# State-space mixer of a two-layer decoder step: outputs by chunk with rows of 64, weights that run on, slots inside the scan

## The chip, the cores and the metric

The kernel runs on one core of one Trainium2 chip. The metric is the device time of one execution in microseconds (us), as the median of several runs.

## What is computed

One inference step of a two-layer decoder, all in fp32, over 288 tokens (a prompt of 256 and 8 sample sequences of 4) and 16 learned meta tokens. Layer 0 mixes tokens with a gated short convolution, layer 1 with a diagonal complex state-space mixer (S5) and a gated linear unit (GLU); each layer ends in an MLP with a squared ReLU. The part that matters here is the mixer of layer 1:

```python
bu_re = jnp.einsum('btgc,gpc->btgp', u32, bbar_re)
bu_im = jnp.einsum('btgc,gpc->btgp', u32, bbar_im)
cum_ar, cum_ai, cum_br, cum_bi = lax.associative_scan(
    _scan_combine, (a_re, a_im, bu_re, bu_im), axis=1)
...
y = (jnp.einsum('gcp,btgp->btgc', c_re, h_re)
     - jnp.einsum('gcp,btgp->btgc', c_im, h_im)
     + d_skip.reshape(SSM_GROUPS, SSM_GROUP_WIDTH) * u32)
g = jax.nn.gelu(y.reshape(bsz, L, D_MODEL))
out = (g @ w_a) * jax.nn.sigmoid(g @ w_b)
```

There are 128 groups of 16 channels, 64 complex states each; `w_a` and `w_b` are 2048 x 2048.

## The kernel before, in words

Activations lie transposed: 16 tiles of 128 channels, with the tokens along the free dimension (304 columns, 288 without the meta tokens). Tokens come in chunks of four, 76 chunks, and the state-space mixer works on chunks: a tile holds 8 groups, as 4 pairs `q` of two groups.

**Weights.** Every dense product takes its weights from one stream, `WeightStream` (lines 41 to 77). A slot is 2 k-tiles by 512 columns, 512 KB: a DMA on the SP queue into one of 4 `raw` buffers (L55), a rounded copy `whi` on ScalarE (L66), the remainder `wlo` on VectorE (L68), 3 buffers of each, then 24 matmuls on TensorE (L200 to L202). `take()` prepares 2 slots ahead and loads 4 more. `W.limit` is the last slot that may be loaded: before the mixer it is set to the end of layer 0's MLP (L1147), and lifted at L1213, once the mixer has begun.

**The mixer**, per tile `t` of 16. `st_m1` (L1036): 8 fp32 matmuls of 128x128 by 76 columns bring the inputs into state space. `st_samples` (L1051, L1052): two small copies on ScalarE. `st_scan` on VectorE: rotate (L1064, L1065, L1067), scan (L1069), rotate back (L1071, L1072, L1074, L1076); `between(k)` puts other work between these steps. `st_y`: 16 fp32 matmuls (L1101, with the tile's inputs) and 32 (L1106, with its states), each with 32 columns of weights that write one strip of 32 partitions of `ybank`, so that the outputs come out with channels on partitions. Then ScalarE takes the gelu (L1113) and its rounded part (L1116), VectorE the remainder (L1117).

**Early slots.** While the tiles run, GLU slots are taken as soon as their k-tiles exist: `run_slots(PERSTEP)` takes up to 2 per tile, after the whole scan and ahead of `st_y`. A slot is gated by `ready`, the number of tiles whose gelu is written. `EARLY` lists the groups and how many k-tiles each takes there: 27 of the 64 GLU slots; the other 37 (`LATE`) follow the mixer.

The order is written by hand: each engine, and each DMA queue, works through its instructions in the program's order.

```python
    for t in range(NT):
        st_samples(t)
        ...
        st_scan(t, between)
        run_slots(PERSTEP)
        lo_of_tile.append(st_y(t))
    lo_of_tile.pop()()
    ready[0] = NT
    run_slots(99)
    st_scan_samples()
```

Of the kernel before, what the change touches and what calls it, by code (L numbers as in the profile page):

```python
# [79 lines left out]
def build(ctx, tc, I, O, dbg=None):  # L80
    nc = tc.nc
    V, S, G, T = nc.vector, nc.scalar, nc.gpsimd, nc.tensor
# [866 lines left out]
    ssm = {}  # L949
    gh = [None, None]  # L950

    def ssm_alloc():
# [3 lines left out]
        blk = xr[:, 0:5120].rearrange("p (n m) -> p n m", m=P)
        ssm["m1"] = [blk[:, 8 * i:8 * i + 8, :] for i in range(2)]
        ssm["m2"] = [blk[:, 16 + 8 * i:24 + 8 * i, :] for i in range(2)]
        ssm["tt"] = [blk[:, 32 + 4 * i:36 + 4 * i, :] for i in range(2)]
        ssm["rot"] = [xr[:, 5120 + i * 816:5120 + (i + 1) * 816] for i in range(3)]  # L960
        ssm["tmp"] = [xr[:, 7568 + i * 544:7568 + (i + 1) * 544] for i in range(3)]
        sel = ssm["sel"] = xr[:, 9200:9712].rearrange("p (j m) -> p j m", j=4)
# [9 lines left out]
        G.memset(xr[:, 0:5120], 0.0)  # L972
# [110 lines left out]
    def st_scan_samples():  # L1083
# [10 lines left out]
    def st_y(t):  # L1094

        def cols_of(ap, i):
            return ap.rearrange("p (x i) -> p x i", i=4)[:, :, i]

        for i in range(4):
            for q in range(4):  # L1100
                T.matmul(out=ybank[32 * q:32 * q + 32, i * NK:(i + 1) * NK], lhsT=cols_of(ssm["tt"][t % 2][:, q, :], i),  # L1101
                         rhs=ssm["U"][:, t * 4 + q, :], start=i == 0, stop=False)
        for r in range(2):
            for i in range(4):
                for q in range(4):
                    T.matmul(out=ybank[32 * q:32 * q + 32, i * NK:(i + 1) * NK],  # L1106
                             lhsT=cols_of(ssm["m2"][t % 2][:, q * 2 + r, :], i), rhs=ssm["S"][t % 2][:, q, r, :],
                             start=False, stop=r == 1 and i == 3)
# [107 lines left out]

    for t in range(NT):
        st_samples(t)

        def between(k):  # L1220
            if k == 0:
                if t + 1 < NT:
                    st_m1(t + 1)
                if t == 0:
                    W.dma_to(W.idx + NRAW)
                while lo_of_tile:
                    lo_of_tile.pop()()
                    ready[0] = t
            elif k == 1 and t + 2 < NT:
                scale_u(t + 2)  # L1230
            elif k == 2 and t < 2:
                W.prep_to(W.idx + 1 + t)
# [121 lines left out]
```

## Time and profile before

| | |
|---|---|
| median of 3 runs | 2567.64 us (2564.65 to 2569.97) |
| the profiled execution's own time | 2565.84 us |
| its span in the trace | 2563.8 us |
| mean granted TensorE clock | 0.973 |
| busy: TensorE, VectorE, ScalarE, GpSimd | 95%, 60%, 37%, 5% |

Line numbers (L200) are those of the kernel before, unless the text says of the kernel after; PE is TensorE's matmuls, PEld its weight loads, DVE VectorE, ACT ScalarE, POOL GpSimd, SP the engine whose queue issues most DMAs. An idle time in brackets stands ahead of an instruction, with what ended it; "issue" means that the trace shows nothing that was waited for. A fp32 matmul shows as two records of PE, a transposition and a matmul on split weights (fp32r) as one.

### The profile page before, as it was taken

How to read it: one execution, taken by the hardware profiler on the slowest of the kernel's cores; microseconds unless marked ns; L12 is line 12 of the kernel's file. 1: busy time of each engine (PE TensorE's matmuls, PEld its weight loads, DVE VectorE, ACT ScalarE, POOL GpSimd, SP SyncE). 2: the span in 40 equal slices, each digit the busy share in tenths (PEclk: the TensorE clock that was granted, in tenths of full speed). 3: DMA queues.
4: the chain of work that ended last, by engine and by line, in shares of the span. 5: the costliest groups of instructions: out<-in, count | busy, mean ns of one | idle time of the engine just before them, and what ended most of it. 6: DMA issues, size and time to landing. Idle time of an engine off the chain costs nothing.

```text
span 2563.8 us, 45558 instructions
## 1 busy us (share of the span) xinstructions
PE 2448.2 (95%) x19176; PEld 2429.6 (95%) x19176; DVE 1533.8 (60%) x2302; ACT 958.1 (37%) x1209; POOL 135.4 (5%) x239
## 2 busy tenths in 40 slices
PE   6999999999998999999996878999999999999998
PEld 6999999999998999999996877999999999999998
DVE  5654556885757765777645556567555545555555
ACT  4333334434433333333432322444333333333334
POOL 2000000000101210000300001000000000000000
PEclk9999999999999999999996888999999999999999
DMA  6555555556665766666678553555555555555554
GB/s 151 155 158 161 159 157 169 148 149 190 177 200 169 209 208 187 203 198 202 206 197 155 166 142 98 166 164 164 165 165 170 159 173 165 165 167 168 164 168 111
DMA packets 260425, 432.46 MB, mean 169 GB/s; under 512 B 65044, under 2 KB 68820, under 8 KB 260188
## 3 DMA queue, kind: packets, MB, share of 16 engines
q1 hardware_dynamic: 250752, 396.30, 53.5%
q0 software_dynamic: 9408, 33.20, 5.2%
q8 instruction: 150, 2.46, 0.4%
q14 instruction: 55, 0.45, 0.1%
q10 hardware_dynamic: 60, 0.05, 0.0%
HBM read 400.44 MB, written 29.05 MB: 168 GB/s over the span
## 4 chain that ended last, share of the span: by engine, by line
PE 51%; issue 1%; ACT 1%; DMA 1%; DVE 1%; SPq 0%; DVEq 0%; ACTq 0%
PE banks L200 16%; PE banks L202 16%; PE banks L201 16%; PE banks L1036 2%; PE banks L1106 1%; PE banks L1101 0%; DMA raw<-in_ssm_glu_w_a 0%; PE banks L1318 0%; DMA ssm_xr<-d_rot 0%; ACT gt L1113 0%; ACT g L1116 0%; DMA raw<-in_mlp_w_down 0%; SPq L1012 0%; DVE wlo L68 0%; ACT whi L66 0%
## 5 line engine op out<-in xcount | busy, mean ns | idle before, releaser
L68 DVE TENSOR_TENSOR wlo<-raw,whi 128x1024 fp32r<-128x1024 f32 x704 | 862.7, 1226 | 824.3 <-ACT whi L66 822.5
L66 ACT ACTIVATE whi<-raw 128x1024 fp32r<-128x1024 f32 x704 | 742.6, 1056 | 993.6 <-PE banks L201 835.9
L200 PE MATMUL banks<-hid,whi 128*128 128x304 f32 (+1 forms) x2048 | 612.2, 299 | 15.3 <-DVE h L876 13.4
L202 PE MATMUL banks<-hid,wlo 128*128 128x304 f32 (+1 forms) x2048 | 611.4, 299 | 1.9 <-DVE wlo L68 1.8
L202 PE MATMUL banks<-xs_m,wlo 128*128 128x304 f32 (+1 forms) x2048 | 611.8, 299 | 0.7 <-DVE wlo L68 0.7
L201 PE MATMUL banks<-hid,whi 128*128 128x304 f32 (+1 forms) x2048 | 612.0, 299 | 0.0
L201 PE MATMUL banks<-xs_m,whi 128*128 128x304 f32 (+1 forms) x2048 | 611.0, 298 | 0.0
L200 PE MATMUL banks<-xs_m,whi 128*128 128x304 f32 (+1 forms) x2048 | 610.9, 298 | 0.0
L200 PEld LDWEIGHTS banks<-hid,whi 128*128 128x128 f32 x2048 | 385.9, 188 | 17.5 <-DVE h L876 14.9
L202 PEld LDWEIGHTS banks<-hid,wlo 128*128 128x128 f32 x2048 | 386.7, 189 | 2.9 <-DVE wlo L68 2.9
L202 PEld LDWEIGHTS banks<-xs_m,wlo 128*128 128x128 f32 x2048 | 385.3, 188 | 1.6 <-DVE wlo L68 1.6
L200 PEld LDWEIGHTS banks<-xs_m,whi 128*128 128x128 f32 x2048 | 385.3, 188 | 1.4 <-issue 0.4
L201 PEld LDWEIGHTS banks<-hid,whi 128*128 128x128 f32 x2048 | 386.0, 188 | 0.0
L201 PEld LDWEIGHTS banks<-xs_m,whi 128*128 128x128 f32 x2048 | 385.3, 188 | 0.1
L200 PE MATMUL banks<-xs,whi 128*128 128x304 f32 x768 | 233.5, 304 | 4.2 <-DVE h L391 4.2
L202 PE MATMUL banks<-xs,wlo 128*128 128x304 f32 x768 | 233.3, 304 | 0.0
L201 PE MATMUL banks<-xs,whi 128*128 128x304 f32 x768 | 232.7, 303 | 0.0
L814 ACT ACTIVATE hid<-at 128x304 fp32r<-128x304 f32 (+1 forms) x128 | 57.8, 451 | 302.1 <-DVE at L921 302.1
L200 PE MATMUL banks<-g,whi 128*128 128x288 f32 x512 | 163.1, 318 | 0.5 <-ACT vy L1198 0.5
L201 PE MATMUL banks<-g,whi 128*128 128x288 f32 x512 | 160.1, 313 | 0.0
L202 PE MATMUL banks<-g,wlo 128*128 128x288 f32 x512 | 159.7, 312 | 0.0
L200 PEld LDWEIGHTS banks<-xs,whi 128*128 128x128 f32 x768 | 145.7, 190 | 4.5 <-DVE h L391 4.4
(255 smaller groups left out, 2304.2 us busy)
## 6 DMA issues: line engine op xcount, KB each, us to landing
raw<-in_mlp_w_up SPq DMA_DIRECT2D x256, 512.0 KB, 3.7
raw<-in_mlp_w_down SPq DMA_DIRECT2D x256, 512.0 KB, 3.7
raw<-in_conv_w_in SPq DMA_DIRECT2D x96, 512.0 KB, 3.9
raw<-in_conv_w_out SPq DMA_DIRECT2D x32, 512.0 KB, 3.7
raw<-in_ssm_glu_w_a SPq DMA_DIRECT2D x32, 512.0 KB, 3.6
raw<-in_ssm_glu_w_b SPq DMA_DIRECT2D x32, 512.0 KB, 3.7
ssm_xr<-d_m SPq DMA_DIRECT2D x64, 128.0 KB, 2.9
d_rot<-prep POOLq DMA_DIRECT2D x8, 816.0 KB, 4.3
```

The lines of the kernel that those rows point to most:

```text
L66: self.nc.scalar.activation(out=hi, in_=r, func=AF.Copy)
L68: eng.tensor_tensor(out=lo, in0=r, in1=hi.bitcast(F32), op=ALU.subtract)
L200: T.matmul(out=o, lhsT=wh, rhs=xh, start=si == 0 and kk == 0, stop=False)
L201: T.matmul(out=o, lhsT=wh, rhs=xl, start=False, stop=False)
L202: T.matmul(out=o, lhsT=wl, rhs=xh, start=False, stop=si + 2 >= len(kts) and kk == 1)
L814: S.activation(out=dh, in_=src, func=AF.Copy)
L1036: T.matmul(out=xbank[:, q, r * NK:(r + 1) * NK], lhsT=m[:, q * 2 + r, :], rhs=ssm["U"][:, t * 4 + q, :], start=True, stop=True)
L1106: T.matmul(out=ybank[32 * q:32 * q + 32, i * NK:(i + 1) * NK], lhsT=cols_of(ssm["m2"][t % 2][:, q * 2 + r, :], i), rhs=ssm["S"][t % 2][:, ...
```

## The change

1. **Outputs by chunk.** The outputs of a tile come out with the 76 chunks on partitions. `st_t(t)` multiplies the tile's inputs (8 matmuls, weights of 64 rows by 76 columns, 64 moving columns), `st_y(t)` its states (16 matmuls of the same form); rows 0 to 63 and 64 to 127 of the array take the two groups of a pair, and write two PSUM banks. ScalarE copies the result out of PSUM (two copies of 76x256), and `st_c(t)` transposes it back with 4 transpositions ahead of the gelu. `m2` and `tt` need no zero blocks any more, and `m2` comes with one DMA in place of two.
2. **Weights run on.** `W.limit`, and the calls that loaded the first GLU slots by hand, go: during the last slots of layer 0's MLP the stream loads and splits GLU slots.
3. **Order.** `st_samples` moves into `between(0)`; `between(1)` now holds the first half of the tile's slots, the transpositions and gelu of the tile before (from tile 3 on), the next tile's `st_m1`, and `st_t`; `between(2)` the other half of the slots. `PERSTEP` becomes a table by tile, 25 early slots and 39 late ones in place of 27 and 37. One PSUM bank fewer serves the early groups (4 for 5).
4. **Matmuls on ones**, whose result nobody reads: 12 in place of 5 ahead of the mixer, and 10 in each of tiles 0 and 1.

```diff
-WP = 5
+WARM = 10
+WP = 12
-EARLY = [(("a", 0), 2), (("b", 1), 2), (("a", 1), 4), ...
+EARLY = [(("a", 0), 2), (("b", 1), 2), (("a", 1), 2), ...
-PERSTEP = 2
+PERSTEP = (0, 0, 1, 1, 2, 2, 1, 2, 1, 2, 2, 2, 2, 2, 2, 2)
...
     def load_m2(t):
-        for g2, g in enumerate(HALF):
-            nc.sync.dma_start(out=ssm["m2"][t % 2][g, :, g], in_=d_m2[t, g2].rearrange("x q r p -> x (q r) p"))
+        nc.sync.dma_start(out=ssm["m2"][t % 2], in_=d_m2[t].rearrange("g x q r p -> (g x) (q r) p"))
...
-    ybank = banks[:, 3072:3584]
-    GBANK = (0, 1, 2, 3, 7)
+    ybank = [banks[:NK, 3072 + g * 512:3328 + g * 512] for g in range(2)]
+    cbank = xbank[:, :, 2 * NK:3 * NK]
+    GBANK = (0, 1, 2, 3)
...
+    def st_t(t):
+        for q in range(4):
+            for g2, g in enumerate(HALF):
+                T.matmul(out=ybank[g2][:, q * 64:(q + 1) * 64], lhsT=ssm["U"][g, t * 4 + q, :], rhs=ssm["tt"][t % 2][g, q, :],
+                         start=q == 0, stop=False)
...
+    def st_y(t):
+        for n in range(8):
+            q, r = n // 2, n % 2
+            for g2, g in enumerate(HALF):
+                T.matmul(out=ybank[g2][:, q * 64:(q + 1) * 64], lhsT=ssm["S"][t % 2][g, q, r, :], rhs=ssm["m2"][t % 2][g, n, :],
+                         start=False, stop=n == 7)
...
+        y = ssm["yt"][t % 2].rearrange("k (i q g e) -> k g i q e", i=4, q=4, g=2)
+        for g2 in range(2):
+            S.activation(out=y[:, g2], in_=ybank[g2].rearrange("k (q e i) -> k i q e", q=4, i=4), func=AF.Copy)
+    def st_c(t):
+        y = ssm["yt"][t % 2].rearrange("k (i x) -> k i x", i=4)
+        for i in range(4):
+            T.transpose(out=cbank[:, i, :], in_=y[:, i, :], identity=ident[:NK, :NK])
...
-    W.limit = end0
     mlp(lambda: xs_mlp, N0, MLP, ssm_pre)
...
     for t in range(NT):
-        st_samples(t)
+        n = PERSTEP[t]
         def between(k):
             if k == 0:
+                st_samples(t)
...
+            elif k == 1:
+                if t + 2 < NT:
+                    scale_u(t + 2)
+                k = run_slots((n + 1) // 2)
+                if t > 2:
+                    lows.append(st_c(t - 1))
+                if t + 1 < NT:
+                    st_m1(t + 1)
+                st_t(t)
+                warm(WARM if t < 2 else 0)
+            elif k == 2:
+                run_slots(n // 2)
         st_scan(t, between)
-        run_slots(PERSTEP)
-        lo_of_tile.append(st_y(t))
+        while lows:
+            lows.pop()()
+        st_y(t)
```

TensorE's order at the mixer's start, from the norm's sum (L1157, L1170 after) to tile 2's `st_m1`; L1098 is `st_t`, L1108 `st_y`, L1121 the transposition, L1225 and L263 matmuls on ones:

```order
-L1157 MATMUL banks<-acc,ssm_xr 128x76 x4
-L263 MATMUL banks<-ones 128x128 x5
+L1170 MATMUL banks<-acc,ssm_xr 128x76 x4
+L263 MATMUL banks<-ones 128x128 x12
 L1036 MATMUL banks<-ssm_big,ssm_xr 128x76 x16
-L1101 MATMUL banks<-ssm_big,ssm_xr 32x76 x16
-L1106 MATMUL banks<-vy,ssm_xr 32x76 x32
+L1098 MATMUL banks<-ssm_xr,ssm_big 76x64 x8
+L1225 MATMUL banks<-ones 128x128 x10
+L1108 MATMUL banks<-ssm_xr,vy 76x64 x16
+L1121 MATMUL banks<-ident,ssm_xr 128x76 x4
 L1036 MATMUL banks<-ssm_big,ssm_xr 128x76 x8
```

48 strip matmuls of a tile became 24, with 10 on ones between them and 4 transpositions behind.

VectorE's order in one tile with two slots, before:

```order
L1064 TENSOR_TENSOR ssm_xr<-banks,ssm_xr 128x544
L1065 TENSOR_TENSOR ssm_xr<-banks,ssm_xr 128x544
L1117 TENSOR_TENSOR g_13685<-gt,g_13685 128x288
L1067 TENSOR_TENSOR ssm_xr<-ssm_xr 128x544
L1167 TENSOR_TENSOR ssm_big<-ssm_big,rstd_82 128x304
L1069 SCALAR_TENSOR_TENSOR ssm_xr<-vy,ssm_xr 128x544
L1071 TENSOR_TENSOR ssm_xr<-ssm_xr 128x544
L1072 TENSOR_TENSOR ssm_xr<-ssm_xr 128x544
L1074 TENSOR_TENSOR vy<-ssm_xr 128x8x67
L1076 TENSOR_TENSOR ssm_big<-ssm_xr 128x4x2
L68 TENSOR_TENSOR wlo<-raw,whi 128x1024 x2
```

And after (L69 is `wlo`, L1128 the gelu's remainder, L1180 the scaling of the inputs):

```order
L1064 TENSOR_TENSOR ssm_xr<-banks,ssm_xr 128x544
L1065 TENSOR_TENSOR ssm_xr<-banks,ssm_xr 128x544
L1067 TENSOR_TENSOR ssm_xr<-ssm_xr 128x544
L1180 TENSOR_TENSOR ssm_big<-ssm_big,rstd_82 128x304
L69 TENSOR_TENSOR wlo<-raw,whi 128x1024
L1069 SCALAR_TENSOR_TENSOR ssm_xr<-vy,ssm_xr 128x544
L69 TENSOR_TENSOR wlo<-raw,whi 128x1024
L1071 TENSOR_TENSOR ssm_xr<-ssm_xr 128x544
L1072 TENSOR_TENSOR ssm_xr<-ssm_xr 128x544
L1074 TENSOR_TENSOR vy<-ssm_xr 128x8x67
L1076 TENSOR_TENSOR ssm_big<-ssm_xr 128x4x2
L1128 TENSOR_TENSOR g_13689<-gt,g_13689 128x288
```

The two splits of weights moved from behind the scan's chain to both sides of the scan (L1069), and the gelu's remainder from inside the chain to its end.

SP's queue at the end of layer 0's MLP, before (L998 writes the mixer's inputs to memory, L1006 reads them back by groups, L1012 loads `m1`):

```order
L55 DMA raw<-in_mlp_w_down 128x2x512
L998 DMA d_u<-h 128x304 x3
L1006 DMA ssm_big<-d_u 16x32x76 x8
L998 DMA d_u<-h 128x304 x8
L1006 DMA ssm_big<-d_u 16x32x76 x8
L1012 DMA ssm_xr<-d_m_189 64x8x64 x2
L55 DMA raw<-in_ssm_glu_w_a 128x2x512
```

And after:

```order
L56 DMA raw<-in_mlp_w_down 128x2x512
L998 DMA d_u<-h 128x304
L56 DMA raw<-in_ssm_glu_w_a 128x2x512
L998 DMA d_u<-h 128x304
L56 DMA raw<-in_ssm_glu_w_b 128x2x512
L998 DMA d_u<-h 128x304
L1006 DMA ssm_big<-d_u 16x32x76 x8
L56 DMA raw<-in_ssm_glu_w_a 128x2x512
L998 DMA d_u<-h 128x304
L56 DMA raw<-in_ssm_glu_w_b 128x2x512
L998 DMA d_u<-h 128x304
L56 DMA raw<-in_ssm_glu_w_b 128x2x512
```

Six loads of GLU weights stand among the writes and reads of the mixer's inputs, where before the first stood behind all of them.

## Rows read from the trace of the kernel before

**Rows 1.** The page: busy time, share of the span and instructions of each engine.

```profile
PE 2448.2 (95%) x19176; PEld 2429.6 (95%) x19176; DVE 1533.8 (60%) x2302; ACT 958.1 (37%) x1209; POOL 135.4 (5%) x239
```

**Rows 2.** Stretches (start:end, length, busy us by engine, clock, DMA, GB/s): the mixer.

```profile
1361.10:1407.70 46.60, 23.64 (x284) 21.78 (x283) 22.82 (x40) 11.39 (x24) 0.00 (x0) 0.58 0.85 156
1407.70:1591.40 183.70, 152.14 (x2027) 148.39 (x2027) 102.49 (x146) 56.89 (x115) 3.23 (x3) 0.84 0.51 142
1591.40:1611.30 19.90, 14.99 (x161) 13.67 (x160) 14.32 (x13) 6.95 (x13) 8.82 (x6) 0.74 0.25 80
1611.30:1730.20 118.90, 118.87 (x897) 118.88 (x898) 72.76 (x107) 53.98 (x74) 2.52 (x4) 1.00 0.56 165
...
1640.00:1700.00 60.00, 60.00 (x455) 60.00 (x454) 37.82 (x58) 27.39 (x37) 0.00 (x0) 1.00 0.56 166
```

**Rows 3.** Timeline (start us, length, what, idle before): the mixer's first tiles.

```profile
1367.27 2.79 PE L1036 MATMUL banks<-ssm_big,ssm_xr 128*128 128x76 f32 x16 [2.04 <-DVE ssm_big L1167]
...
1377.32 1.26 SPq L55 DMA_DIRECT2D raw<-in_ssm_glu_w_a  x1
...
1384.35 1.06 ACT L66 ACTIVATE whi<-raw 128x1024 fp32r<-128x1024 f32 x1 [13.80 <-DMA raw<-in_ssm_glu_w_a]
1385.43 1.23 DVE L68 TENSOR_TENSOR wlo<-raw,whi 128x1024 fp32r<-128x1024 f32 x1 [11.30 <-ACT whi L66]
...
1402.90 0.72 DVE L1064 TENSOR_TENSOR ssm_xr<-banks,ssm_xr 128x544 f32<-128x544 f32 x1 [3.49 <-ACT ssm_big L1051]
...
1407.77 0.59 PE L200 MATMUL banks<-g,whi 128*128 128x288 f32 x1
```

**Rows 4.** Timeline: tile 13's start to tile 14's, the pattern of each tile.

```profile
1560.10 0.41 ACT L1113 ACTIVATE gt<-banks 128x288 f32<-128x288 f32 x1 [3.60 <-PE banks L1106]
...
1561.21 0.72 DVE L1064 TENSOR_TENSOR ssm_xr<-banks,ssm_xr 128x544 f32<-128x544 f32 x1 [3.45 <-ACT ssm_big L1051]
...
1562.67 3.50 PE L1036 MATMUL banks<-ssm_big,ssm_xr 128*128 128x76 f32 x16 [2.63 <-issue]
...
1574.14 0.61 PEld L1101 LDWEIGHTS banks<-ssm_big,ssm_xr 128*32 128x32 f32 x32 [0.17 <-issue]
...
1574.72 1.24 PE L1106 MATMUL banks<-vy,ssm_xr 128*32 128x76 f32 x64
...
1577.13 0.72 DVE L1064 TENSOR_TENSOR ssm_xr<-banks,ssm_xr 128x544 f32<-128x544 f32 x1 [3.88 <-ACT ssm_big L1051]
```

**Rows 5.** Waits (waiter <- releaser: us in total, times, longest), 1361 to 1612 us.

```profile
DVE ssm_xr L1064 <- ACT ssm_big L1051: 58.5, 16, 3.9
```

**Rows 6.** Stretches: TensorE behind the gap of Rows 4, and later in that tile.

```profile
1562.70:1569.60 6.90, 6.90 (x31) 6.90 (x32) 5.74 (x9) 1.60 (x2) 0.00 (x0) 0.51 0.09 20
1569.80:1574.10 4.30, 4.30 (x34) 4.18 (x32) 1.23 (x1) 1.06 (x1) 0.00 (x0) 1.00 0.36 115
```

**Rows 7.** Timeline of PE: groups of fp32 matmuls at the full clock.

```profile
1363.90 1.32 PE L263 MATMUL banks<-ones 128*128 128x128 f32 x10
...
1420.96 1.98 PE L1036 MATMUL banks<-ssm_big,ssm_xr 128*128 128x76 f32 x16 [2.63 <-issue]
...
2546.11 0.68 PE L1307 MATMUL banks<-one,acc 128*72 128x1 f32 x8 [1.57 <-DVE acc L327]
2546.66 7.16 PE L1318 MATMUL banks<-ident,xf 128*72 128x128 f32 x64
```

**Rows 8.** DMA issues (KB each, median us to landing) and rate, 1345 to 1390 us.

```profile
DMA packets 14146, 8.44 MB, mean 188 GB/s; under 512 B 10875, under 2 KB 12516, under 8 KB 14144
...
ssm_big<-d_u SPq DMA_DIRECT2D x16, 152.0 KB, 9.3
...
raw<-in_ssm_glu_w_a SPq DMA_DIRECT2D x3, 512.0 KB, 7.8
```

**Rows 9.** The scan's line (min/median/max ns), and PE in the last tile.

```profile
L1069 DVE TENSOR_TENSOR_SCAN ssm_xr<-vy,ssm_xr x16: 1280/1282/2255, 1372.9 to 1595.5; 128x544 f32<-128x544 f32 x16
...
1601.96 1.36 PE L1106 MATMUL banks<-vy,ssm_xr 128*32 128x76 f32 x34 [4.44 <-issue]
```

More of the change, by code (lines that the diff above doesn't have):

```diff
@@ L31 @@
 BGOFF = 14
+WARM = 10
 ULAG = 2
-WP = 5
-EARLY = [(("a", 0), 2), (("b", 1), 2), (("a", 1), 4), (("b", 2), 4), (("a", 2), 6), (("b", 3), 8), (("a", 3), 12),
+WP = 12
+EARLY = [(("a", 0), 2), (("b", 1), 2), (("a", 1), 2), (("b", 2), 4), (("a", 2), 6), (("b", 3), 8), (("a", 3), 10),
          (("b", 0), 16)]
 LATE = [(n, c) for n, c in EARLY[:-1]]
-PERSTEP = 2
+PERSTEP = (0, 0, 1, 1, 2, 2, 1, 2, 1, 2, 2, 2, 2, 2, 2, 2)
 class WeightStream:
@@ L131, in build @@
     wmlp(0)
-    end0 = len(slots)
     gname = {"a": "ssm_glu_w_a", "b": "ssm_glu_w_b"}
@@ L955, in ssm_alloc @@
         b = ssm["big"] = rp.tile([P, 12000], F32, tag="BIG", name="ssm_big")
[L956 to L962, printed above, removed]
+        ssm["m1"] = [xr[:, i * 1024:(i + 1) * 1024].rearrange("p (n m) -> p n m", m=P) for i in range(2)]
+        ssm["m2"] = [xr[:, 2048 + i * 512:2560 + i * 512].rearrange("p (n m) -> p n m", m=64) for i in range(2)]
+        ssm["tt"] = [xr[:, 3072 + i * 256:3328 + i * 256].rearrange("p (n m) -> p n m", m=64) for i in range(2)]
+        ssm["rot"] = [xr[:, 3584 + i * 816:3584 + (i + 1) * 816] for i in range(3)]
+        ssm["tmp"] = [xr[:, 6032 + i * 544:6032 + (i + 1) * 544] for i in range(3)]
+        ssm["yt"] = [xr[:NK, 7664 + i * 512:8176 + i * 512] for i in range(2)]
+        sel = ssm["sel"] = xr[:, 8688:9200].rearrange("p (j m) -> p j m", j=4)
         ssm["S"] = [vy[:, i * 608:(i + 1) * 608].rearrange("p (q r k) -> p q r k", q=4, r=2) for i in range(2)]
@@ L971, in ssm_alloc @@
         ssm["fin"] = [b[:, 9472:10624], b[:, 10624:11776]]
-        G.memset(xr[:, 0:5120], 0.0)
+        G.memset(xr[:, 0:2048], 0.0)
         G.memset(vy, 0.0)
@@ L1014, in load_m2 @@
     def load_m2(t):
-        for g2, g in enumerate(HALF):
-            nc.sync.dma_start(out=ssm["m2"][t % 2][g, :, g], in_=d_m2[t, g2].rearrange("x q r p -> x (q r) p"))
+        nc.sync.dma_start(out=ssm["m2"][t % 2], in_=d_m2[t].rearrange("g x q r p -> (g x) (q r) p"))
     def load_t(t):
         for g2, g in enumerate(HALF):
-            nc.sync.dma_start(out=ssm["tt"][t % 2][g, :, g],
+            nc.sync.dma_start(out=ssm["tt"][t % 2][g],
                               in_=d_t.rearrange("j c g e i -> (j c) g (e i)")[:, t * 8 + g2:t * 8 + 8:2, :])
@@ L1092, in st_scan_samples @@
             G.tensor_tensor(out=d, in0=d, in1=x, op=ALU.add)
[L1094 to L1108, printed above, removed]
+    def st_t(t):
[3 more added lines that the diff above has]
+                         start=q == 0, stop=False)
@@ L1112, in st_y @@
+    ready = [0]
+    def st_c(t):
+        y = ssm["yt"][t % 2].rearrange("k (i x) -> k i x", i=4)
+        for i in range(4):
+            T.transpose(out=cbank[:, i, :], in_=y[:, i, :], identity=ident[:NK, :NK])
         gt = tp.tile([P, N0], F32, tag="eb", name="gt")
-        S.activation(out=gt[:, :N1].rearrange("p (i k) -> p i k", i=4),
-                     in_=ybank[:, :N0].rearrange("p (i k) -> p i k", i=4)[:, :, NM:], func=AF.Gelu_apprx_tanh)
+        S.activation(out=gt[:, :N1].rearrange("p (i k) -> p i k", i=4), in_=cbank[:, :, NM:], func=AF.Gelu_apprx_tanh)
@@ L1115, in st_y, with lo @@
         gt_hi, gt_lo = g_at(t)
         S.activation(out=gt_hi, in_=gt[:, :N1], func=AF.Copy)
-        return lambda: V.tensor_tensor(out=gt_lo, in0=gt[:, :N1], in1=gt_hi.bitcast(F32), op=ALU.subtract)
+        def lo():
+            V.tensor_tensor(out=gt_lo, in0=gt[:, :N1], in1=gt_hi.bitcast(F32), op=ALU.subtract)
+            ready[0] = t + 1
+        return lo
     def g_at(t):
@@ L1182, in early @@
             for _ in range(4):
-                k = GBANK[nbank[0] % 5]
+                k = GBANK[nbank[0] % 4]
                 nbank[0] += 1
@@ L1194, in early @@
                     a = pslot[n, mg] * 4 + i
-                    assert a < 16 or (a - 15) * N1 <= ready[0] * 4 * NK
+                    assert a < 16 or (a - 15) * N1 <= outs[0] * 4 * NK
                     S.activation(out=part[:, a, :], in_=ps[i][:, :N1], func=AF.Copy)
@@ L1198, in early @@
                     S.activation(out=ssm["sg"][i], in_=ps[i][:, :N1], func=AF.Sigmoid)
-    ready = [0]
+    outs = [0]
     work = early()
@@ L1207, in run_slots, with warm @@
             n -= 1
+        return n
+    def warm(n):
+        for _ in range(n):
+            T.matmul(out=banks[:, 0:P], lhsT=ones, rhs=ones, start=True, stop=True)
     for t in range(2):
@@ L1212, in build @@
     st_m1(0)
-    W.limit = len(slots)
-    W.dma_to(W.idx + 2)
-    lo_of_tile = []
+    lows = []
     for t in range(NT):
-        st_samples(t)
+        n = PERSTEP[t]
         def between(k):
             if k == 0:
+                st_samples(t)
+                if t <= 2:
+                    while lows:
+                        lows.pop()()
+            elif k == 1:
+                if t + 2 < NT:
+                    scale_u(t + 2)
+                k = run_slots((n + 1) // 2)
+                if t > 2:
+                    lows.append(st_c(t - 1))
                 if t + 1 < NT:
                     st_m1(t + 1)
[L1224 to L1232, printed above, removed]
-        st_scan(t, between)
-        run_slots(PERSTEP)
-        lo_of_tile.append(st_y(t))
-    lo_of_tile.pop()()
-    ready[0] = NT
+                st_t(t)
+                warm(WARM if t < 2 else 0)
+            elif k == 2:
+                run_slots(n // 2)
+        st_scan(t, between)
+        while lows:
+            lows.pop()()
+        st_y(t)
+        outs[0] = t + 1
+        if t < 2:
+            lows.append(st_c(t))
+    st_c(NT - 1)()
     run_slots(99)
```

## The prediction

> **What bounds the kernel now.** Three views, in this order. The page's busy shares first: TensorE is busy 95% of the span and no other engine over 60% [rows 1], so time can come only from TensorE's pauses, from stretches at its lower clock, or from fewer and cheaper matmuls. Then the stretches, which show where pauses and lower clock lie: in the mixer, 1361.1 to 1730.2 us, 369.1 us in all [rows 2]. Behind the mixer's last tile TensorE is full at a granted clock of 1.00; ahead of it the clock is 0.58, 0.84 and 0.74, and a good part is idle. Then the timeline, for what each pause waits on.
>
> In the steady tiles it shows one loop. `st_y` ends, ScalarE takes the gelu and behind it the sample copies (its queue is in order), VectorE's first rotation L1064 waits 3.45 to 3.88 us for the copy L1051, and TensorE's next `st_m1` starts after an idle of 2.63 us [rows 4]. L1064 loses 58.5 us so in 16 tiles [rows 5]. The pause costs twice: behind it the clock is 0.51 for 6.9 us and only then 1.00 [rows 6], and the 16 records of L1036 take 3.50 us in place of 1.98 [rows 4, 7]. A tile with two slots lasts 1577.13 - 1561.21 = 15.9 us.
>
> The first slot starts at 1407.77. Ahead of it VectorE stands idle for 11.30 us in tile 0: the split L68 is next in its queue and waits for L66, which waits for a load issued at 1377.32 and rounded at 1384.35 [rows 3]. The scan's second half, `st_y` and tile 1 are all queued behind.
>
> What the stretch behind the first slot holds: 64 slots at 3.17 us (24 x 60/455, from the full stretch [rows 2]) are 202.9 of 1730.2 - 1407.7 = 322.5 us. The other 119.6 us: idle 183.7 - 152.1 = 31.6; lower clock about 27 (0.16 of 152 to 184 us); outputs 14 x (0.61 + 1.24) = 25.9 [rows 4]; `st_m1` 13 x 16 x 0.112 = 23.4 (0.112 is 1.98 us less one record's 0.3, over 15 [rows 7]); the last tile's idle 4.9 and 0.26 x 15 = 3.9. Together 116.7, so 3 us are left unnamed.
>
> **The change part by part.** The 64 slots stay, at the same price. Six other parts move.
>
> (a) The head, from 1361.1 to the first slot.
> - The weights run on: the split of tile 0 finds its slot long loaded and rounded, and the 11.30 us go: -11. At most that; less if the load still comes late (rival B).
> - Seven more matmuls on ones ahead of `st_m1`: ten records in 1.32 us [rows 7] are 0.26 per matmul, 1.8 us, of which TensorE's idle of 2.04 ahead of L1036 [rows 3] hides a part: +1 (0 to 3.7, at half the clock).
> - Ten in tiles 0 and 1: 2.6 us each at the full clock, 5.2 at half. They stand between `st_t` and `st_y`, beside VectorE's scan and rotations back (1.28 + 3 x 0.72, 3.4 us): +4 for both (0 to 7).
> - The first slot moves from behind `st_y` of tile 2's scan, 4.87 us after its L1064 (1402.90 to 1407.77 [rows 3]), into `between(1)`, beside that L1064, since its weights and the two gelus that it needs exist by then: -5 (-3 to -5).
>
> Sum -11.
>
> (b) The steady tiles. Slots now stand ahead of the transpositions, of `st_m1` and of `st_t`, so that TensorE has 3 to 6 us of work while the scan runs, and the gelu of a tile is only wanted a tile later. The pause and with it the low clock go; in their place:
> - `st_m1` as before, 13 x 1.8 = 23.4.
> - Outputs, 14 tiles x 24 matmuls x p. No row has this form. **p** is the term that decides. The nearest row is L1307, with 72 columns of weights and one moving column: eight records 0.55 us apart in all (2546.11 to 2546.66), 68 ns each, 135 per matmul [rows 7]. The other near row is L1106, four partial arrays at a time: 1.24/32 = 39 ns per matmul, 155 per set of four [rows 4]. So parts of the array work side by side, and a set costs what one matmul of L1307's size does; I take two halves in 135 ns, p = 0.068: 22.8 us. Lower end 0.039, if halves pack like strips; upper ends 0.135 (one after the other, rival A) and 0.224 (a whole L1036 each, rival C).
> - Transpositions, 14 x 4 x 0.112 (64 records of L1318 in 7.16 us [rows 7]) = 6.3, at full price, since they are on TensorE.
> - They write into the banks of `st_m1`, which so waits for the gelu: 13 x 0.6 = 7.8 (0.41 is L1113; the hand-over between the engines is put at 0.2, between 0 and the 0.70 that 1561.21 - 1560.10 leave beside it [rows 4]).
> - Changes between whole array and halves, four in a tile. The row ahead of L1101, where the array goes over to strips, shows 0.17 us of idle on the weight load [rows 4], some 0.09 more than its usual spacing: 4 x 0.09 x 14 = 5.0 (0 to 0.17 each: 0 to 9.5). The Trainium skill, "TensorEngine Tiling (Array Packing)", says in its Key Properties that switching modes requires the engine to drain, and "TensorE: Matmul & The Clock Gate" puts a drain at about 175 ns; by that the term would be near 10 and the total 5 us less.
> - Steps between engines that the above misses, 13 x 0.3 = 4; lower clock left over, 5 of the 27 (the tiles with one slot); the last tile, where POOL doubles VectorE's times (the scan 2.255 in place of 1.28) and TensorE idles 4.44 us [rows 9], 7 in place of 8.8.
>
> Sum 23.4 + 22.8 + 6.3 + 7.8 + 5.0 + 4 + 5 + 7 = 81.3 in place of 119.6: -38. A tile with two slots then takes 6.34 + 1.8 + 1.6 + 0.45 + 0.6 + 0.36, about 11.2 us, bound by TensorE. VectorE's work in it is 6 x 0.72 + 1.28 + 2 x 1.23 + about 0.9 (two operations of 288 and 304 columns) = 9.0 us, which leaves 2 us of slack; ScalarE's two copies out of PSUM are off the path, since the transpositions come a tile later. One DMA in place of two for `m2` lies in SP's queue beside a DMA share of 0.51 [rows 2] and costs nothing. Layer 0's last slots are covered likewise: the splits of GLU weights there are work that VectorE does at 60%. The slots after the mixer become 39 from 37 and stay TensorE's.
>
> **Sum.** -11 - 38 = -49 us against the profiled execution's 2565.84: 2517. The median shown lies 1.8 us above that execution, so the forecast is **2519 us**.
>
> **The rivals.**
>
> A. *The halves run one after the other*, so that a matmul costs L1307's whole 135 ns. For: no row shows two halves at once, only strips that split the columns too. Against: L1106's sets. 384 output matmuls x 0.067 = 26 us: -23, **2545 us**. The Trainium skill, "TensorE: Matmul & The Clock Gate", section "LDWEIGHTS (loading the stationary operand)", has a weight load cost its columns over 1.2 in ns, whatever its rows; 76 columns and two records would be 127 ns. L1307's 68 ns a record for 72 columns agrees with that (60). Chance 0.22.
>
> B. *The mixer's inputs come late.* Six GLU loads now stand among the writes and reads of `d_u`. The queues already move 188 GB/s there, the reads land after 9.3 us and the loads after 7.8 [rows 8]; five loads ahead of the last read are 2.6 MB, 13 us: **2532 us**. Against: the loads start earlier by as much as they are spread. Chance 0.10.
>
> D. *VectorE's chain binds.* If 2.9 of today's 3.5 to 3.9 us of wait for L1051 stay beside its 9.0 us, the tile takes 11.9, 0.7 more than TensorE's 11.2: 13 x 0.7 = 9, **2528 us**. Inside the forecast's own range.
>
> C. *The other side: slower.* The output matmuls cost L1036's price of 0.224 each, because a half array with 64 moving columns still takes two whole passes. Then 384 x (0.224 - 0.068) = 60 us are added, -49 + 60 = +11, **2579 us**. It decides from p = 0.068 + 49/384 = 0.196 on. For: all fp32 rows of 128 weight columns show 0.112 a record, whatever moves [rows 7]; against: L1307's 68 ns with fewer columns. Chance 0.06.
>
> No change at all would need p near 0.19, or a loop through the gelu that is as long as before: 0.04.
>
> **How the numbers follow.** The forecast with D has 0.58, A 0.22, B 0.10, C 0.06, no change 0.04. The range of the likeliest goes from 2506 (p at 0.039, -10; switches free, -5) to 2528; up to 2548 it takes in B and A with 3 us beside. Left out are C, no change, and A and B together: 0.1 to 0.2. A measurement of this kernel tells about 0.2% from no change, 5 us; so faster 0.90, same 0.04, slower 0.06.
>
> **What would show it.** In the changed kernel's profile: VectorE's wait ahead of the weight split in tile 0 gone; the first slot some 35 us behind 1361; L1064's wait for the copy under 1 us; a clock near 1.00 from tile 3 on; L1108's records 34 ns apart, so that 16 matmuls take 1.1 us. Records 68 ns apart are A, over 100 ns C. A pause of TensorE ahead of the first `st_m1` with a DMA of `d_u` as its end is B; a pause ahead of `st_y` with L1076 as its end is D. The prediction is wrong if a tile with two slots takes over 14 us, or if the head is not shorter.

## The result and the profile after

| | before | after |
|---|---|---|
| median of the runs | 2568.06 us (2564.65 to 2569.97) | 2520.59 us (2519.83 to 2523.84) |
| ratio | | 0.9819, 95% interval 0.9802 to 0.9836 |
| span of the profiled execution | 2563.8 us | 2519.0 us |
| end of layer 0's MLP (start of L993 on TensorE) | 1361.11 | 1359.07 |
| first GLU slot | 1407.77 | 1400.75 |
| first matmul of layer 1's MLP | 1730.22 | 1684.82 |

The forecast was 2519 us. In the two traces the mixer, from L993 to the MLP, takes 369.1 us before and 325.7 after: 46.7 + 322.4 against 41.7 + 284.1, cut at the first slot. So 43.4 of the span's 44.8 us lie in the mixer: 5.0 in its head, 38.4 behind it.

The page's busy shares, after (answers to [rows 1]):

```profile
PE 2438.4 (97%) x18526; PEld 2418.0 (96%) x18526; DVE 1537.7 (61%) x2302; ACT 965.3 (38%) x1241; POOL 134.6 (5%) x239
```

The stretches, after: head, steady tiles, last tile, rest of the GLU (answer to [rows 2]; the head's row starts at 1361.10, 2.0 us behind L993):

```profile
1361.10:1400.75 39.65, 29.27 (x224) 27.90 (x225) 15.29 (x29) 8.52 (x19) 0.00 (x0) 0.66 0.97 178
1400.75:1543.40 142.65, 133.99 (x1463) 127.46 (x1460) 113.59 (x156) 64.05 (x146) 8.76 (x6) 1.00 0.59 170
1543.40:1565.00 21.60, 16.35 (x121) 15.40 (x120) 11.12 (x11) 7.74 (x13) 5.33 (x3) 0.76 0.27 84
1565.00:1683.00 118.00, 118.00 (x894) 118.00 (x893) 72.26 (x107) 53.90 (x75) 2.52 (x4) 1.00 0.55 168
```

TensorE idles 8.7 of 142.65 us in the steady tiles, where it idled 31.6 of 183.7, and the clock there is 1.00 in place of 0.84. Head and last tile are still idle in part and at a low clock.

The timeline of the mixer's head, after (L1225 are the ten matmuls on ones):

```profile
1367.63 1.91 PE L1036 MATMUL banks<-ssm_big,ssm_xr 128*128 128x76 f32 x16
1371.45 3.69 PE L1036 MATMUL banks<-ssm_big,ssm_xr 128*128 128x76 f32 x16 [1.92 <-ACT ssm_big L1051]
...
1376.28 4.63 PE L1225 MATMUL banks<-ones 128*128 128x128 f32 x20
...
1380.84 1.42 PE L1108 MATMUL banks<-ssm_xr,vy 64*76 64x64 f32 x32
...
1384.71 0.72 DVE L1064 TENSOR_TENSOR ssm_xr<-banks,ssm_xr 128x544 f32<-128x544 f32 x1 [9.13 <-ACT gt L1123]
...
1389.23 3.66 PE L1036 MATMUL banks<-ssm_big,ssm_xr 128*128 128x76 f32 x16 [5.74 <-DMA ssm_xr<-d_m]
...
1394.03 4.46 PE L1225 MATMUL banks<-ones 128*128 128x128 f32 x20
...
1398.43 1.31 PE L1108 MATMUL banks<-ssm_xr,vy 64*76 64x64 f32 x32
...
1400.75 0.38 PE L200 MATMUL banks<-g,whi 128*128 128x288 f32 x1
```

VectorE's 11.30 us of [rows 3] are gone. In their place TensorE waits 5.74 us for the weights `m1` of tile 2, and the ones stand whole between `st_t` and `st_y`, at the lower clock (0.50 and 0.53).

One steady tile with two slots, after (answers to [rows 4]):

```profile
1513.22 1.31 PE L1108 MATMUL banks<-ssm_xr,vy 64*76 64x64 f32 x32
1514.46 0.40 PE L200 MATMUL banks<-g,whi 128*128 128x288 f32 x1
...
1517.75 0.43 PE L1121 MATMUL banks<-ident,ssm_xr 76*128 76x76 f32 x4
1518.67 2.01 PE L1036 MATMUL banks<-ssm_big,ssm_xr 128*128 128x76 f32 x16 [0.50 <-ACT gt L1123]
1520.61 0.76 PE L1098 MATMUL banks<-ssm_xr,ssm_big 64*76 64x64 f32 x16
1521.30 0.40 PE L200 MATMUL banks<-g,whi 128*128 128x288 f32 x1
...
1524.68 1.31 PE L1108 MATMUL banks<-ssm_xr,vy 64*76 64x64 f32 x32
```

The tile lasts 1524.68 - 1513.22 = 11.46 us, where it was 15.9; the only wait of TensorE in it is the half microsecond for the gelu. The waits, after, 1361 to 1570 us, show it in total (answers to [rows 5]):

```profile
DVE ssm_xr L1064 <- ACT gt L1123: 19.7, 2, 10.5
...
PE banks L1036 <- ACT gt L1123: 6.2, 12, 0.5
PE banks L1036 <- DMA ssm_xr<-d_m: 5.7, 1, 5.7
```

L1064's 58.5 us in 16 tiles have become 19.7 in two, tiles 1 and 2.

### The profile page after: what moved, and what is told of

The parts are those of the page before. It is cut to its first block, busy times and chain, and to the rows that moved or that the text cites. A ratio compares the mean times of both kernels' runs of the same rounds, so it can differ in the third digit from the quotient of the medians.

```text
span 2519.0 us, 44232 instructions
## 1 busy us (share of the span) xinstructions
PE 2438.4 (97%) x18526; PEld 2418.0 (96%) x18526; DVE 1537.7 (61%) x2302; ACT 965.3 (38%) x1241; POOL 134.6 (5%) x239
## 4 chain that ended last, share of the span: by engine, by line
PE 51%; DMA 1%; ACT 1%; issue 0%; DVE 0%; SPq 0%; DVEq 0%; ACTq 0%
PE banks L200 16%; PE banks L202 16%; PE banks L201 16%; PE banks L1036 1%; PE banks L1108 1%; DMA d_u<-h 1%; PE banks L1098 0%; DMA ssm_xr<-d_m 0%; PE banks L1342 0%; SPq L1006 0%; ACT gt L1123 0%; PE banks L1225 0%; PE banks L1121 0%; ACT sq L324 0%; ACT ssm_big L1209 0%
## 5 line engine op out<-in xcount | busy, mean ns | idle before, releaser
L69 DVE TENSOR_TENSOR wlo<-raw,whi 128x1024 fp32r<-128x1024 f32 x704 | 864.2, 1228 | 810.7 <-ACT whi L67 809.6
L200 PE MATMUL banks<-g,whi 128*128 128x288 f32 x512 | 154.8, 302 | 0.7 <-ACT g L1125 0.7
L201 PE MATMUL banks<-g,whi 128*128 128x288 f32 x512 | 151.9, 297 | 0.9 <-DVE g L1128 0.9
L202 PE MATMUL banks<-g,wlo 128*128 128x288 f32 x512 | 151.7, 296 | 0.0
```

The costliest lines, as they stand in the source:

```text
L69: eng.tensor_tensor(out=lo, in0=r, in1=hi.bitcast(F32), op=ALU.subtract)
L200: T.matmul(out=o, lhsT=wh, rhs=xh, start=si == 0 and kk == 0, stop=False)
L201: T.matmul(out=o, lhsT=wh, rhs=xl, start=False, stop=False)
L202: T.matmul(out=o, lhsT=wl, rhs=xh, start=False, stop=si + 2 >= len(kts) and kk == 1)
```

## The experiments

Medians are of 4 to 11 runs, and each ratio stands to runs of the kernel before that were taken beside them. The end of layer 0's MLP lies anywhere from 1357.5 to 1367.5 us in the profiles of these kernels, which differ hardly at all ahead of it, so the mixer is compared by its own length too, from L993 to layer 1's MLP, in one profile each:

| kernel | median us | ratio (95% interval) | head | behind the first slot | mixer |
|---|---|---|---|---|---|
| before | 2568.06 | 1 | 46.7 | 322.4 | 369.1 |
| changed | 2520.59 | 0.9819 (0.9802 to 0.9836) | 41.7 | 284.1 | 325.7 |
| e1 no ones in tiles 0, 1 | 2522.00 | 0.9823 (0.9809 to 0.9836) | 38.5 | 286.1 | 324.6 |
| e2 halves in turn | 2538.27 | 0.9889 (0.9875 to 0.9902) | 43.0 | 300.0 | 343.0 |
| e3 transposed elsewhere | 2518.04 | 0.9805 (0.9792 to 0.9819) | 41.9 | 277.1 | 319.0 |
| e4 strips, new order | 2507.78 | 0.9769 (0.9756 to 0.9783) | 40.0 | 270.4 | 310.4 |
| e5 before, weights run on | 2564.60 | 0.9987 (0.9978 to 0.9996) | 43.9 | 320.2 | 364.1 |
| e6 weights gated again | 2526.75 | 0.9840 (0.9826 to 0.9853) | 45.3 | 285.7 | 330.9 |
| e7 old order, new outputs | 2587.47 | 1.0078 (1.0064 to 1.0091) | 46.3 | 342.2 | 388.5 |
| e8 inputs read later | 2516.62 | 0.9805 (0.9791 to 0.9818) | 34.9 | 285.6 | 320.5 |
| e9 = e4 + e8 | 2497.51 | 0.9726 (0.9712 to 0.9739) | 26.8 | 271.8 | 298.6 |
| e10 = e9, no ones | 2496.05 | 0.9722 (0.9709 to 0.9735) | 26.3 | 271.9 | 298.2 |
| e11 = e9, GpSimd last | 2492.76 | 0.9703 (0.9690 to 0.9716) | 28.5 | 265.2 | 293.7 |
| e12 = e10, GpSimd last | 2494.90 | 0.9715 (0.9702 to 0.9728) | 26.1 | 267.8 | 293.9 |

### What carries the gain: the order or the outputs

e7 puts tiles 2 to 15 of the changed kernel back into the old order:

```diff
             if k == 0:
+                if 2 <= t < NT - 1:
+                    st_m1(t + 1)
...
-                k = run_slots((n + 1) // 2)
-                if t > 2:
-                    lows.append(st_c(t - 1))
...
         st_scan(t, between)
-        while lows:
-            lows.pop()()
+        run_slots(n)
+        if t >= 2:
+            st_t(t)
         st_y(t)
-        if t < 2:
-            lows.append(st_c(t))
+        lows.append(st_c(t))
```

> The changed kernel from tile 2 on in the order of before: slots behind the whole scan, then output matmuls, copies, transpositions and gelu at once, and the next st_m1 in between(0). Theory (the order carries the gain): the pause of TensorE is back, longer by the copies and transpositions (about 2 us a tile), with the lower clock behind it; by terms 119.6 + 9 + 27 in place of 81 us, some 50 to 75 more than the changed kernel, 2570 to 2595. Rival (outputs by chunk carry it): 2520 to 2530.

2587.47 us: 67 more than the changed kernel, and more than the kernel before. TensorE's timeline in it:

```profile
1516.54 1.26 PE L1108 MATMUL banks<-ssm_xr,vy 64*76 64x64 f32 x32
1518.53 0.49 PE L1121 MATMUL banks<-ident,ssm_xr 76*128 76x76 f32 x4 [0.73 <-ACT ssm_xr L1114]
1521.25 2.88 PE L1036 MATMUL banks<-ssm_big,ssm_xr 128*128 128x76 f32 x16 [2.23 <-ACT ssm_big L1051]
1523.86 0.59 PE L200 MATMUL banks<-g,whi 128*128 128x288 f32 x1
```

Two pauses, 0.73 for the copies and 2.23 for gelu and samples, and behind them the slow L1036 and slots at 0.59 that the kernel before had too. The order carries the whole gain: behind the first slot, strips take 322.4 us in the old order and 270.4 in the new (e4), outputs by chunk 342.2 and 284.1. The order stands here for all of part 3 of the change, with its table of slots; what each piece of it is worth was not tested.

e4 keeps the order and takes the outputs in strips, with the layout and loads of before:

```diff
-        for q in range(4):
-            for g2, g in enumerate(HALF):
-                T.matmul(out=ybank[g2][:, q * 64:(q + 1) * 64], lhsT=ssm["U"][g, t * 4 + q, :], ...
+        for i in range(4):
+            for q in range(4):
+                T.matmul(out=ybank[32 * q:32 * q + 32, i * NK:(i + 1) * NK], lhsT=cols_of(ssm["tt"][t % 2][:, q, :], i), ...
...
-        for g2 in range(2):
-            S.activation(out=y[:, g2], in_=ybank[g2]...
-        for i in range(4):
-            T.transpose(out=cbank[:, i, :], in_=y[:, i, :], ...
```

> The changed kernel's order and weights with the outputs in strips as before (no copies out of PSUM, no transpositions). Theory (the gain is the order's; outputs by chunk cost TensorE 0.76 + 1.31 + 0.43 us a tile where strips cost 0.61 + 1.24, and bring the wait for the gelu): 14 x 0.65 + 6 = 15 us less than the changed kernel, about 2506. Rival (outputs by chunk are needed: strips hold the clock down or the gelu late): 2521 or more.

2507.78 us, and the mixer 15.4 us shorter than in the changed kernel, 13.7 of them behind the first slot. The theory's size came out, but not by all its terms: it had dearer outputs by chunk as one of them. Counted from start to start of TensorE's records behind the first slot, the outputs take 28.0 us in strips and 27.7 in halves, the same; what goes is 6.0 of transpositions, 6.2 of waiting for the gelu and 1.3 of `st_m1`. TensorE's timeline with strips (a tile with two slots is 10.4 us):

```profile
1510.29 1.29 PE L1109 MATMUL banks<-vy,ssm_xr 128*32 128x76 f32 x64
1514.80 1.90 PE L1036 MATMUL banks<-ssm_big,ssm_xr 128*128 128x76 f32 x16
1516.63 0.76 PE L1100 MATMUL banks<-ssm_big,ssm_xr 128*32 128x76 f32 x32
1520.70 1.29 PE L1109 MATMUL banks<-vy,ssm_xr 128*32 128x76 f32 x64
```

No transpositions and no wait ahead of L1036. With the new order, outputs by chunk are a loss.

### What an output matmul costs

e2 issues the same matmuls, but all of one half of the rows first:

```diff
-        for n in range(8):
-            q, r = n // 2, n % 2
-            for g2, g in enumerate(HALF):
+        for g2, g in enumerate(HALF):
+            for n in range(8):
+                q, r = n // 2, n % 2
```

> The changed kernel with all output matmuls of rows 0 to 63 issued first and then all of rows 64 to 127, so that no two halves can run side by side. Theory (0.070 us per matmul is two at a time, 0.135 each alone): 384 x 0.067 = 26 us more, 2546, and L1108's 32 records take 2.2 us in place of 1.31. Rival (0.070 is the price of one alone and pairs do not overlap): no change, 2520.

TensorE's timeline in it:

```profile
1509.53 1.08 PE L1098 MATMUL banks<-ssm_xr,ssm_big 64*76 64x64 f32 x16
1513.91 2.18 PE L1108 MATMUL banks<-ssm_xr,vy 64*76 64x64 f32 x32
```

68 ns a record, 136 ns a matmul, where the pairs took 1.31 / 32 = 41 ns a record with the end of the last one; from start to start, a pair of records, one of each half, goes out every 68 ns, 34 ns a record. So pairs do run side by side, two in the time of one. The mixer grew by 17.2 us, not 26. The edit does not keep the halves apart wholly: the second half's first record starts at 1514.79 us, and three records of the first half still follow it, so that about 0.2 us of each set runs side by side after all. Up to the start of the next slot, L1098 takes 0.32 us more and L1108 0.87, 1.2 in a tile where the expectation had 24 x 0.067 = 1.6; and the matmuls of tiles 0 and 1 stand beside other waits.

e3 moves the transposed outputs out of the banks of `st_m1`:

```diff
-    cbank = xbank[:, :, 2 * NK:3 * NK]
+    cfree = banks[:, 3072:4096].rearrange("p (g x) -> p g x", g=2)[:, :, 256:256 + 2 * NK]
+    cbank = [cfree[:, i // 2, (i % 2) * NK:(i % 2 + 1) * NK] for i in range(4)]
...
```

> The changed kernel with the transposed outputs in the free half of the two output banks, so that st_m1 no longer shares banks with what the gelu reads. Theory (st_m1 waits for that): the 12 waits of 0.50 to 0.54 us go, 6 us less, 2514 to 2515. Rival (the scan's chain on VectorE is next, or the wait goes over to the output matmuls): 2519 to 2521.

In the trace the 12 waits are gone (one of 0.5 us is left, ahead of the output matmuls), and the stretch behind the first slot is 7.0 us shorter. The median fell by 2.5 us only, less than the theory has and more than the rival: all four runs (2512.56 to 2518.97) lie below the changed kernel's four, but the intervals of the two ratios overlap, and in its profile layer 0 ended 5.4 us later than in the changed kernel's. The waits of TensorE behind the first slot name the next in line, VectorE's chain, 3.8 us of it in the last tile:

```profile
PE banks L1110 <- DVE vy L1076: 7.3, 6, 3.8
```

### The head

e1 takes the ones out of tiles 0 and 1:

```diff
-                warm(WARM if t < 2 else 0)
+                warm(0)
```

> The changed kernel without the ten matmuls on ones in tiles 0 and 1. Theory (they lie on the path: 4.6 us in tile 0, 4.5 in tile 1, where st_y waits for them and for nothing else): tile 0's are hidden again, since tile 1's st_m1 load of m1 lands only at 1389 us; tile 1's 4.5 us go; the first slot runs some 20 matmuls at the lower clock, +2 to 3. So about 2 us less than the changed kernel, near 2518.5. Rival (the ones buy the clock for longer than they cost): 2 to 6 us more, 2523 to 2527.

The timeline of TensorE:

```profile
1374.13 1.31 PE L1108 MATMUL banks<-ssm_xr,vy 64*76 64x64 f32 x32 [1.48 <-DVE ssm_big L1076]
...
1387.95 3.67 PE L1036 MATMUL banks<-ssm_big,ssm_xr 128*128 128x76 f32 x16 [11.04 <-DMA ssm_xr<-d_m]
...
1396.10 0.59 PE L200 MATMUL banks<-g,whi 128*128 128x288 f32 x1
```

Head 3.2 us shorter, the rest 2.0 longer: the first slots run at a granted clock of 0.50 for 6.4 us, where the changed kernel has 1.00. The medians can't be told apart, so the 2 us that were expected do not show. Tile 0's ones were hidden, since the wait for `m1` grows from 5.74 to 11.04 us when they go.

e8 moves the second read of the mixer's inputs, which tiles 8 to 15 use, behind `m1` on SP's queue:

```diff
     flush()
-    u_in(8, NT)
...
     st_m1(0)
+    u_in(8, NT)
```

> The changed kernel with the second read of the mixer's inputs (tiles 8 to 15) put behind tile 2's m1 load on SP's queue. Theory (m1 is late because it is queued behind that read, which waits for the last writes): TensorE's wait of 5.7 us ahead of tile 2's st_m1 goes, 2514 to 2516. Rival (the DMA engines are full, and m1 lands as late from any place in the queue): 2519 to 2522.

SP's queue in the changed kernel:

```profile
1365.51 3.70 SPq L998 DMA_DIRECT2D d_u<-h  x5
1374.24 6.04 SPq L1006 DMA_DIRECT2D ssm_big<-d_u  x8
1380.38 5.44 SPq L1012 DMA_DIRECT2D ssm_xr<-d_m  x4
```

and in e8, with TensorE's `st_m1` of tile 2:

```profile
1371.23 1.20 SPq L1012 DMA_DIRECT2D ssm_xr<-d_m  x2
1375.80 5.95 SPq L1006 DMA_DIRECT2D ssm_big<-d_u  x8
...
1384.30 3.70 PE L1036 MATMUL banks<-ssm_big,ssm_xr 128*128 128x76 f32 x16 [2.97 <-ACT ssm_big L1051]
```

In the changed kernel the queue stands from 1369.2 to 1374.2 until the writes have landed, and `m1` behind it; moved ahead, it goes out at 1371.23, and the wait of 5.74 us becomes 2.97, for the sample copies. The head is 6.8 us shorter, the stretch behind it 1.5 longer, the median 4.0 less; the runs of the two kernels overlap, so the head shows it and the median alone would not.

e5 takes the limit from the kernel before, e6 puts it back into the changed kernel:

```diff
-    W.limit = end0
     mlp(lambda: xs_mlp, N0, MLP, ssm_pre)
...
-    W.limit = len(slots)
-    W.dma_to(W.idx + 2)
...
```

> The kernel before with the limit on the weight stream taken away, and nothing else. By the sum on record VectorE's stall of 11.3 us in tile 0 goes: 2557. New theory, from the run without ones (there TensorE waited 11.0 us for tile 2's m1, which stands on SP's queue behind the second read of the mixer's inputs): the stall only comes back as that wait, since m1 lands near 1389 us whatever VectorE does; 3 to 5 us gained, 2563 to 2565.

> The changed kernel with the limit on the weight stream and the loads by hand put back. By the sum on record: 11 us more, 2531. New theory (in tile 0 the stall for the weights lies beside 4.6 us of matmuls on ones and 5.7 us of waiting for m1): 0 to 4 us more, 2520 to 2525.

e5: 2564.60 us, 3.4 us less than the kernel before, the mixer 5.0 us shorter. VectorE's 11.3 us are gone, and TensorE waits in tile 1 in their place:

```profile
1397.06 3.66 PE L1036 MATMUL banks<-ssm_big,ssm_xr 128*128 128x76 f32 x16 [12.50 <-DMA ssm_xr<-d_m]
```

e6: 2526.75, 6.2 us more than the changed kernel; neither the 11 of the sum nor the 0 to 4 of the new theory. Its VectorE and TensorE:

```profile
1382.14 1.23 DVE L69 TENSOR_TENSOR wlo<-raw,whi 128x1024 fp32r<-128x1024 f32 x1 [12.68 <-ACT whi L67]
...
1385.54 2.29 PE L1109 MATMUL banks<-ssm_xr,vy 64*76 64x64 f32 x32 [9.68 <-DVE ssm_big L1077]
...
1391.98 3.69 PE L1037 MATMUL banks<-ssm_big,ssm_xr 128*128 128x76 f32 x16 [2.68 <-ACT ssm_big L1052]
```

The stall is back and reaches TensorE past the ones, while `m1` is no longer waited for. Taking the stall away thus brings the other wait with it, and SP's queue shows how. In the kernel before:

```profile
1361.47 3.72 SPq L998 DMA_DIRECT2D d_u<-h  x4
1368.26 5.97 SPq L1006 DMA_DIRECT2D ssm_big<-d_u  x8
```

and in e6 (L1007 is the same read):

```profile
1363.99 5.93 SPq L1007 DMA_DIRECT2D ssm_big<-d_u  x8
```

The second read goes out 7.2 and 6.5 us behind L993 there (1361.11 and 1357.48), but 15.2 behind it in the changed kernel (1374.24 to 1359.07) and 15.5 in e5, where the six GLU loads stand among the writes that it waits for. Tile 2's `m1`, behind the read in the queue, lands 22.4 us behind L993 in e6, 30.0 in the changed kernel and 31.3 in e5.

### A version that beats both

e9 joins e4 and e8; e10 leaves out the ones in it; e11 holds GpSimd's work on the samples back, by one operation that reads the last gelu's remainder; e12 is all of it.

```diff
     run_slots(99)
+    lo15 = g_at(NT - 1)[1].bitcast(F32)
+    G.tensor_tensor(out=ssm["st"][0][:, :N1], in0=lo15, in1=lo15, op=ALU.mult)
     st_scan_samples()
```

> Strips in the new order, with the second read of the mixer's inputs behind tile 2's m1 load. Theory: of the 11.5 us that TensorE waits for m1 in the run with strips, some 3 stay as the wait for the sample copies (2.97 in the run with the read moved alone): 8 less than strips alone, about 2500. Rival (the head is bound by the writes and reads of the mixer's inputs): 2505 or more.

> The same without the matmuls on ones in tiles 0 and 1. Theory (with m1 in time, the ones are on the path in both tiles, 3.4 + 3.2 us, of which VectorE's chain hides some 2, and the first slots run at the lower clock, 2 to 3 us): 1 to 3 us less than with them, 2497 to 2499. Rival (the clock is worth more): 2 to 4 more, 2502 to 2504.

> Strips, the read moved, and GpSimd's work on the samples held back until the last tile's gelu remainder is written (one more GpSimd operation reads it). Theory (GpSimd's operations lengthen VectorE's in tiles 14 and 15: the scan 2.39 for 1.28, a split 2.25 for 1.23, L1071 and L1072 1.78 for 0.72, and TensorE waits 4.63 us for that): some 4 us less than without, about 2496. Rival (GpSimd's work then lengthens the splits of the late slots, and TensorE waits there): no change, 2500.

> Strips, the read moved, no ones in tiles 0 and 1, GpSimd's work held back. Theory: the gains add, 2492 to 2495. Rival (without the ones the lower clock reaches into the first tiles and takes it back): 2498 to 2500.

e9: 2497.51 us, 10 less than e4; the head lost 13 us, more than the wait for `m1`, as in e9 L1064 waits for no gelu (6.21 and 6.73 us in e8). e10 differs from it by less than the runs can tell. e11: 2492.76, the mixer 4.9 us shorter than in e9, with 6.6 less behind the first slot and 1.6 more in the head, which the edit does not touch. The waits of TensorE, e9:

```profile
PE banks L1109 <- DVE vy L1074: 6.2, 4, 4.6
```

and e11, with the scan's line (min/median/max ns), whose longest was 2380 in e9:

```profile
PE banks L1109 <- DVE vy L1074: 1.7, 4, 0.5
...
L1069 DVE TENSOR_TENSOR_SCAN ssm_xr<-vy,ssm_xr x16: 1282/1284/1285, 1377.5 to 1520.4; 128x544 f32<-128x544 f32 x16
```

Behind the shorter wait the clock does not fall: around the last tile it is 0.81 in e9 (1518 to 1545 us) and 1.00 in e11 (1521 to 1545). In its place TensorE waits 1.7 us for GpSimd's results later (L1269, the final states).

e12's 2494.90 can't be told from e11. The best version, e11, is 28 us below the changed kernel; it keeps the change's order and weights, and drops its outputs.

## Why the prediction was right, and where it was not

The forecast of 2519 us was 1.6 below the median. A part of that nearness is luck: the two profiled executions lie 44.8 us apart, and the mixer gained 43.4 in them, where 49 were summed; but the median of before lies 2.2 us above its profiled execution, and the changed kernel's 0.4 below its own. The parts:

- **The steady tiles: right.** -38 on record, -38.4 measured, for all that lies behind the first slot. p was put at 0.068; pairs of records go out 68 ns apart, 0.068 a matmul, and e2 shows that this is two at a time. Outputs and changes of form were 22.8 + 5.0 = 27.8 us by the sum, 27.7 in the trace; the wait for the gelu 7.8 and 6.2; the tile 11.2 and 11.46. Both of the two rows taken as nearest for p held: L1307's price for one, L1106's sets for the side by side. Two terms came out by luck. The transpositions were 6.3 and 6.0 us, but they go out 65 ns apart and not 112, and the end of the last one, for which the gelu waits, makes up the rest. And the 5 us of lower clock left over were not needed (1.00 in the steady tiles), while the slots took 210.6 us for 202.9, a part of it at the last tile's lower clock.
- **The drain.** The two weighings of the change of form were 0.09 and 0.175 us each. The trace has 0.09 at each of the four: 0.22 from the last slot matmul to L1108 (1513.00 to 1513.22) where slot matmuls follow each other at 0.13, 0.20 from L1036 to L1098 where L1036's records follow at 0.11, and 0.16 from L1098 and from L1108 to the slot behind where theirs follow at 0.07. Here the measurement goes with the row. The Trainium skill says that changing the tiling mode drains TensorE ("TensorEngine Tiling (Array Packing)", Key Properties), and has a drain at about 175 ns ("TensorE: Matmul & The Clock Gate", Single matmul latency); the gap measured here is half of that.
- **What the sum held and did not say.** Its own terms for outputs by chunk, 22.8 + 6.3 + 5.0 + 7.8 = 41.9, against 25.9 for the strips of before, made them a loss within the gain of 38. Not of 16 us, since strips in the new order pay the changes of form too: e4 has 28.0 us of outputs. The transpositions and the wait are what differs, 14.1 on record, and e4's stretch behind the first slot is 13.7 shorter. The prediction bundled them with the order, so that the reader saw one gain where there was a larger one and a loss.
- **The head: the step that failed.** The sum had -11 for it, with the first slot some 35 us behind the head's start; it is 5.0 shorter, 41.7 us. "The weights run on: ... the 11.30 us go: -11" was true of VectorE and not of the path: alone it is worth 3.4 us of the median and 5.0 of the mixer (e5). In the stall's place came the wait for tile 2's `m1`, and the change itself made it: the GLU loads among the writes send the second read of the inputs out 8 us later, and `m1` stands behind that read (e5, e6, e8). Rival B saw the queue and its crowd, but put the wait on the inputs ahead of the first `st_m1`, and costed it as bandwidth; it came at tile 2's `st_m1`, from the place in the queue. Of the smaller terms, the seven more matmuls on ones cost the 1 us of the sum (`st_m1` starts 5.3 us behind the norm's sum, before 4.3), but that sum came 1.4 us later behind L993, a wait for VectorE that no term had; and the first slot moved ahead as forecast, from 4.87 us behind tile 2's L1064 to 0.7 ahead of it.
- **The ones.** "+4 for both" were 4.6 + 4.4 us, at the lower clock and all between `st_t` and `st_y`. Tile 0's cost nothing while `m1` was late, tile 1's bought the clock for the first slots at its own price (e1): no net time either way.
- **The last tile.** 7 us on record, where the kernel before had 8.8; 9.2 by the stretch, so it gained nothing (5.25 idle, 0.24 of 16.35 busy). That GpSimd lengthens VectorE's operations there is shown by e11.
- **The rivals.** A is the price of the halves in turn, which e2 made real, and not what the change does. C's 0.224 did not come near. D was not the bound, but is next: once 7 us leave TensorE in e3, five tiles ahead of the last one wait for VectorE's chain, 3.5 us in all, 1.5 of it in tile 14.

## What to carry to other kernels

When a stall goes because transfers start earlier, follow every queue past it: what the early transfers now stand ahead of, and what is issued behind a transfer that waits, decides how much of the stall is gained, and moving one transfer can be worth as much as removing the stall. When a change bundles an order and a new form of the work, write their terms apart: here the order gave more than the whole, the form took some back, and the old form in the new order beat both. Work that only lies beside the critical path, such as GpSimd's here, still belongs where the engine that it slows, here VectorE, has slack.

## What the runs showed of the hardware that was not expected

- Code that the kernels share took a different time in each profile: layer 0's MLP ended between 1357.5 and 1367.5 us. A difference of 3 us between medians of four runs may be no more than this; the length of the changed stretch itself shows more.
- The ones do what they are for (granted clock 1.00 in place of 0.50 for the first slots), and what they give is no more than they take: without them the head is 3.2 us shorter and the rest 2.0 longer (e1).
- With GpSimd's operations out of the way, the scan takes 1282 to 1285 ns in all 16 tiles; beside them the last tile's took 2354 in the changed kernel.
- Matmuls on two halves of the rows run side by side when they are issued in alternation, a pair of records every 68 ns; issued one half after the other, a single record takes 68 ns (e2).
